# Spreading a relative-position bias over the query rows: four copies out of one SBUF partition, or one round trip through DRAM

## The chip, the cores and the metric

The kernel runs on one core of a Trainium2 chip. The metric is the device time of one execution in microseconds (us), lower is better. Engines are called as the profile calls them: PE is the matrix engine (PEld its weight loads), DVE the vector engine, ACT the scalar engine, POOL the general one, SP the engine that only issues transfers (SPq is its queue). A DMA is a transfer; its landing is the moment at which its completion is signalled.

## The reference

A small model is computed in one launch: two blocks of width 1024 over 256 tokens, about 210 MB of float32 weights. What matters here is the first mixer, a differential attention with 4 heads. Its scores get a bias that depends on the distance of query and key alone:

```python
buckets = t5_bucket(jnp.arange(S, dtype=jnp.int32))
bias_dist = rel_bias.astype(jnp.float32)[buckets].T          # [4 heads, 256 distances]
...
dist = qpos[:, None] - kpos[None, :]
causal = dist >= 0
bias = bias_dist[:, jnp.clip(dist, 0, S - 1)]
s = jnp.einsum('bqhd,bkhd->bhqk', q, k).astype(jnp.float32) * scale + bias
s = jnp.where(causal, s, -jnp.inf)
```

Two such softmaxes (of two halves of each head) are subtracted from each other with a factor lambda, and the result weights the values. Everything after it (cross-attention, MLP, a gated convolution, the second block) is left as it is by the change.

## The kernel before

**Products.** Each activation and each weight is split into two float32r parts, hi and lo, and each product is three matmuls of 128x256: `hi*x_hi`, `hi*x_lo`, `lo*x_hi` (`mm3`, L192; all matmuls stand on L189). A `pair` (L487) is 2 blocks of 128 output features by 8 blocks of depth, so 48 matmuls, from one weight tile of 1 MB.

**The stream of weights.** A list fixed at build time (`plan`) holds all tiles in the order of their use: for the first mixer q, k, q, k (tiles 0 to 3), u, u (tiles 4, 5), v, v (6, 7), then those of the cross-attention's keys. A tile is loaded by SP into one of four staging buffers (`stg`, L297), cast to `hi` by ACT in two halves (L319), and DVE subtracts `lo = stg - hi`, also in halves (L198, in `prep_next`). When DVE has read a staging buffer, SP may load the tile four places later into it. PE and SP run in the order in which the program is written; the order on DVE, ACT and POOL is set by a scheduler at build time.

**SP's queue.** All loads of this kernel but two small ones are issued by SP, one after the other. An issue that has to wait (for a buffer, for data, or for the completion of the eighth DMA before it, whose semaphore it reuses) holds back all that stand behind it.

**The prologue** (`setup`, L342) issues x, tiles 0 to 3, the memory (`memr`, twice 512 KB), the pooling weights (`poolw`) and small constants, and then, in `diff_setup`, the bias. That function takes a one-hot table (`oh`, 33 x 384, loaded in `diff_load`) and multiplies it with `rel_bias` on PE, which gives a row of 384 values for each head: at place j the bias of distance 255 - j, and -1e30 from place 256 on. DVE copies it to SBUF as `be` (L574, 4 partitions, one for each head). Query row p of a head needs 256 values that begin at place 127 - p. So for each head one DMA reads 128 overlapping stretches of 1 KB out of the one partition that holds the head's row, and writes one to each of the 128 partitions of `bias` (L576 to L580):

```python
for h in range(4):
    row = e[h:h + 1, :]
    nc.sync.dma_start(
        out=self.bias[:, h, :],
        in_=bass.AP(row.tensor, row.offset + P - 1, [list(row.ap[0]), [-1, P], [1, T]]))
```

**The use.** `diff_scores` (L598) is called for heads 0 and 1 after the fourth tile's product, for heads 2 and 3 later. For each of two softmaxes and two stretches of keys (256 for the second half of the queries, 128 for the first) one DVE instruction adds the bias to the scores in PSUM and takes the maximum (L613, 16 of them in all, 4 for a head). ACT takes the exponentials, DVE normalises and subtracts (L623 to L630). Then PE turns the weights (`diff_T`, L635 to L637), ACT copies them to SBUF as `pt` (L639), and `diff_out` multiplies them with the values.

**Beside it** POOL forms window sums of `pu`, which DVE writes from the u products (L198 `pu<-g,r`); their temporaries `pwt` share two buffers (tag `sq`) with `pt`, so `pt` of the first head waits until POOL is done with them.

**PE's order** around this place: q, k, q, k, scores of heads 0 and 1 (`a<-dqk`), the two u pairs, a small mean, the first v product, `diff_T` of head 0, the scores of head 2, `diff_out` of head 0, and so on.

Of the kernel before, what the change touches and what calls it, by code (L numbers as in the profile page):

```python
# [10 lines left out]
F32 = mybir.dt.float32  # L11
# [6 lines left out]
P = 128  # L18
# [12 lines left out]
# columns of the table of parameter vectors, 128 values to a column  # L31
# [15 lines left out]
# matrices of weights, cut into tiles of k blocks of 128 rows by n columns  # L47
# [8 lines left out]
def _tiles(a, k, n):  # L56
    """[layers, rows, columns] to [layers, row tile, column tile, partition, k * n]"""
    l, r, c = a.shape
    a = a.reshape(l, r // (k * P), k, P, c // n, n).transpose(0, 1, 4, 3, 2, 5)
    return np.ascontiguousarray(a).reshape(l, r // (k * P), c // n, P, k * n)  # L60


def _layout(inputs):
    """weights by tiles, activations and parameter vectors with features on partitions"""
    out = {}
    for name, (k, n) in TILES.items():
        a = np.asarray(inputs[name])
        if name == "w_in_2":
            gate = a[:, :, 4 * 512:4 * 512 + P]
            out["w_in_2_ff"] = _tiles(gate, k, P)  # L70
            a = np.concatenate([a[:, :, :2048], a[:, :, 2056:]], axis=2)
        out[name] = _tiles(a, k, n)
    # the modulation's weights with output features on partitions
    a = np.asarray(inputs["w_ada_2"])[0].T.reshape(24, 2, P, D)
    out["w_ada_2"] = np.ascontiguousarray(a.transpose(0, 2, 1, 3)).reshape(24, P, 2 * D)
    out.update(_vectors(inputs))
    out["rel_bias"] = np.ascontiguousarray(inputs["rel_bias"])
    out["pool_w"] = np.ascontiguousarray(np.asarray(inputs["pool_w"])[0].transpose(1, 0, 2))
    return out
# [17 lines left out]
def _constants():  # L97
    eye = np.eye(P, dtype=np.float32)
    blk = np.zeros((P, P), np.float32)
    blk[:64, :64] = 1.0 / 64  # L100
    blk[64:, 64:] = 1.0 / 64
    inv = np.zeros((P, 4, 16), np.float32)
    for g, w in enumerate((2, 4, 8, 16)):
        inv[:, g, :] = np.float32(1) / np.minimum(np.arange(16) + 1, w).astype(np.float32)
    small = np.concatenate([eye, blk, inv.reshape(P, 64)], axis=1)

    n = np.arange(T)
    nf = np.maximum(n, 1).astype(np.float32)
    large = 16 + (np.log(nf / np.float32(16)) / np.float32(math.log(8.0))
                  * np.float32(16)).astype(np.int32)  # L110
    bucket = np.where(n < 16, n, np.minimum(large, 31))
    onehot = np.zeros((33, 384), np.float32)
    for j in range(384):
        if j < 256:
            onehot[bucket[255 - j], j] = 1.0
        else:
            onehot[32, j] = NEG

    pos = np.arange(T, dtype=np.float32)
    inv_freq = np.float32(10000.0) ** (-np.arange(0, P, 2, dtype=np.float32) / np.float32(P))  # L120
    ang = (pos[None, :] * inv_freq[:, None]).astype(np.float32)
    cos = np.cos(ang).astype(np.float32)
    sin = np.sin(ang).astype(np.float32)
    rope = np.concatenate([np.concatenate([cos, cos]), np.concatenate([-sin, sin])], axis=1)
    dec = np.zeros((P, 4, T), np.float32)
    for h in range(4):
        lg = math.log(1.0 - 2.0 ** (-5.0 - h))
        d = np.arange(T)[None, :] - np.arange(P)[:, None]
        dec[:, h, :] = np.where(d >= 0, np.exp(np.maximum(d, 0) * lg) * P ** -0.5, 0.0)
    sel = np.zeros((P, 8), np.float32)  # L130
    for h in range(8):
        for part in range(3):
            sel[32 * part + h, h] = 1.0
    mask = np.where(np.arange(P)[:, None] >= np.arange(P)[None, :], 0.0, -(2.0 ** 100))
    late = np.concatenate([rope, dec.reshape(P, 4 * T), sel, mask], axis=1)
    return {"k_small": small.astype(np.float32), "k_onehot": onehot,
            "k_late": late.astype(np.float32)}


class Operand:  # L140
    """an activation, features on partitions, as the sum of two float32r parts"""
# [16 lines left out]
class Kernel:  # L158
# [53 lines left out]
    def w(self, key, name, l, c0, ncol):  # L212
        """256 columns at a time of a matrix of 1024 rows"""
        for c in range(c0 // T, (c0 + ncol) // T):
            self.order.append((key, self.a[name][l, 0, c], 256, 8))
# [33 lines left out]
    def plan_ada(self, start, j, span, n=12):  # L249
        """n loads of the modulation's weights among the items from start"""  # L250
# [34 lines left out]
    def dma_next(self, part=None, parts=4):  # L285
        """the next weights from DRAM, all of them or a part"""
# [131 lines left out]
    def norm_mean(self, acc, parts=False):  # L418
        """mean of squares over D, on every partition: PSUM [P, T]"""
# [11 lines left out]
    def rsqrt(self, out, m, scratch, scale=1.0, gain=1.0, eps=EPS):  # L431
        """out = gain * (scale * m + eps) ** -0.5: a guess by exp and ln, and one Newton step"""
# [31 lines left out]
    def norm_columns(self):  # L464
        """1 / 16 of the norm's scale as columns by token: [P, 2]"""
# [7 lines left out]
    def r_columns(self, r, c=None):  # L473
        """r [P, T], the same on every partition, as columns by token: [P, 2]"""
# [11 lines left out]
    def pair(self, key, x, ko=False, bank=None, start=True, stop=True, k0=0, k1=8, w=None,  # L486
             mid=None):  # L487
        """two blocks of 128 output features: [P, 2, T]"""
# [12 lines left out]
    def halves(self, key, x, k0):  # L501
        """four pairs: the blocks of x from k0 for all of them first, then the others"""
# [10 lines left out]
    def natural(self, key, x, w=None):  # L513
        """[token, 2, 256 output features] with tokens on partitions"""
# [14 lines left out]
    def residual(self, i, v, col, last_norm=None):  # L529
        """h += v for pair i, then the next module's operands"""  # L530
        hp = self.h[:, 2 * i:2 * i + 2, :]
        self.tt(hp, v, hp, ALU.add)
        self.make_x(i, hp, col)
        self.norm_add(i, hp)

# [31 lines left out]
    def diff_setup(self):  # L567
        """the bias by distance, then its band for every query row; lambda"""
# [7 lines left out]
        for h in range(4):  # L576
            row = e[h:h + 1, :]
            nc.sync.dma_start(
                out=self.bias[:, h, :],
                in_=bass.AP(row.tensor, row.offset + P - 1, [list(row.ap[0]), [-1, P], [1, T]]))  # L580
# [17 lines left out]
    def diff_scores(self, h):  # L598
# [11 lines left out]
        spans = ((slice(0, 256), slice(0, 256)), (slice(256, 384), slice(128, 256)))  # L610
        for j in range(2):
            for b, (c, bc) in enumerate(spans):
                nc.vector.tensor_tensor_reduce(out=e[:, j, c], in0=bks[j][:, c],  # L613
                                               in1=self.bias[:, h, bc], op0=ALU.add, op1=ALU.max,
# [64 lines left out]
    def pool_windows(self):  # L679
        """means over windows, less the token itself"""  # L680
# [7 lines left out]
    def pool_step(self, i):  # L688
        """the windows of pair i of the groups"""
# [368 lines left out]
    def ada_row(self):  # L1058
        """silu(c) on every partition"""
# [20 lines left out]
    def shift_cols(self, part):  # L1080
        """the shift as one more column of the operand (and a column of zeros)"""
# [9 lines left out]
    def z_block(self, v, r, dst, bcol):  # L1091
        """dst = v * r, and what the shift adds to it as a column"""
# [30 lines left out]
    def last_of_first(self, i, v):  # L1123
        """the end of the first block: h, and operands for both norms that follow"""
# [6 lines left out]
    def norm_double(self):  # L1131
        """r1 of the final norm, and r12 = r1 * r2, r2 of the norm of what the first gives:
        r2 = (r1 * r1 * m2 + eps) ** -0.5, so r12 = (m2 + eps * (m1 + eps)) ** -0.5"""
# [15 lines left out]
    def two(self, key, x, ko=False, bank=None, mid=None):  # L1149
        """two blocks of output features, each [P, T + 2] in its own bank"""  # L1150
# [11 lines left out]
    def head_rms(self, qk, i, bcol, gain):  # L1162
        """rms over the 64 features of a head, two heads to a block; pair i of qk in place"""
# [16 lines left out]
    def forget(self, v, r):  # L1180
        """cumulative log forget gates, in three bf16 parts whose sum is exact"""
# [9 lines left out]
        # ln(1 + a): a guess, and one Newton step l + (1 + a) * exp(-l) - 1  # L1191
# [15 lines left out]
    def to_natural(self, v2, r, dst, c0):  # L1207
        """two blocks with features on partitions to tokens on partitions: dst [P, 2, c0:c0+2P]"""
# [29 lines left out]
    def gate(self, v2, r, dst, silu):  # L1238
# [6 lines left out]
        # -1 / (1 + exp(-z)): a guess by exp and ln, and one Newton step  # L1245
# [44 lines left out]
    def weighted(self, bk, pt, v, cs, start, stop):  # L1290
        """rows of queries: bk [P, 2, n] from weights pt (keys on partitions) and v"""
# [4 lines left out]
    def fox_out(self, g, pts):  # L1296
        """heads 2g and 2g+1"""
# [13 lines left out]
    def mix_scale(self, o, rr, n):  # L1311
        """o (tokens on partitions, n heads) times rr"""
# [17 lines left out]
    def mix_gate(self, vs, i, part, gname, gates):  # L1330
        """turned heads, times gain and gate: pair i of a part of the operand"""
# [41 lines left out]
    def second_mixer(self):  # L1373
# [84 lines left out]
        # what goes between the two blocks of a pair, and what after it  # L1458
# [92 lines left out]
    def finish(self, i, v):  # L1551
        """the last residual, and out"""
# [75 lines left out]
```

## Time and profile before

| what | value |
|---|---|
| runs of the kernel before | 1122.46, 1122.86, 1123.25 us, median 1122.86 |
| the profiled execution | span 1120.5 us from its first to its last instruction, on core 0 |
| median of the runs less that span | 2.4 us |
| PE busy | 1094.8 us, 98% of the span |
| DVE, ACT, POOL busy | 772.2, 579.5, 122.8 us (69%, 52%, 11%) |
| moved by DMA | 217.75 MB, mean 194 GB/s |

The page gives of the profiled execution its span alone; the runs were timed apart from it, and their median is 2.4 us longer than the span, which is what lies around it. A time taken out of the span or added to it is carried over to the median as it is. PE is busy nearly all the time, but a PE that is busy can still run at either of two clock levels, which the profile gives as the granted clock (1.00 or 0.50).

### The profile page before, as it was taken

What the parts mean: (1) busy time and instruction counts of PE and PEld (TensorE: products, weight loads), DVE (VectorE), ACT (ScalarE), POOL (GpSimd) and SP (SyncE); (2) the same over time, 40 slices, a digit from 0 to 9 for tenths busy, and PEclk for the clock granted to TensorE, in tenths of its full rate; (3) what the DMA queues carried; (4) which work ended last, traced back from release to release, by engine and by line L of the source; (5) the groups of instructions that cost most, each with busy time, mean ns of one, the idle gap of its engine ahead of it and who ended that gap; (6) DMA issues with size and microseconds to landing.
All of it is one profiled execution on the core that took longest, in us unless ns stands there. A gap on an engine that the chain in (4) does not pass through costs nothing.

```text
span 1120.5 us, 21438 instructions
## 1 busy us (share of the span) xinstructions
PE 1094.8 (98%) x9043; PEld 1084.8 (97%) x9043; DVE 772.2 (69%) x1173; ACT 579.5 (52%) x934; POOL 122.8 (11%) x113
## 2 busy tenths in 40 slices
PE   7789999999999999999999999999999999999998
PEld 6689999999999999999999999999999999999998
DVE  6497666886666686674659877656986679555552
ACT  6465554654444464454546544446766657544441
POOL 4130100200000020110001000003222012111110
PEclk9899999999999999999999999999999999999999
DMA  8845454487666555555428877644543335545521
GB/s 254 234 156 186 147 192 145 164 324 256 251 255 256 220 181 188 188 189 188 151 77 334 320 288 275 256 153 171 189 151 114 113 114 197 217 177 183 178 103 39
DMA packets 32747, 217.75 MB, mean 194 GB/s; under 512 B 3683, under 2 KB 4748, under 8 KB 7308
## 3 DMA queue, kind: packets, MB, share of 16 engines
q1 hardware_dynamic: 32560, 216.34, 54.2%
q8 instruction: 71, 1.16, 0.4%
q14 instruction: 24, 0.20, 0.1%
q10 hardware_dynamic: 92, 0.05, 0.0%
HBM read 214.80 MB, written 1.05 MB: 193 GB/s over the span
## 4 chain that ended last, share of the span: by engine, by line
PE 90%; DVE 4%; DMA 3%; ACT 1%; POOL 1%; issue 1%; SPq 0%; DVEq 0%; ACTq 0%; POOLq 0%
PE g L189 59%; PE a L189 30%; DMA stg<-in_ab_w_in_dram 2%; DVE lo L198 2%; DVE xl L201 1%; POOL pwt L198 1%; ACT hi L319 1%; DMA h<-in_xT_dram 0%; POOL acc L198 0%; ACT sq L205 0%; PE a L873 0%; DVE h L201 0%; DVE h L198 0%; PE a L1220 0%; PE a L1326 0%
## 5 line engine op out<-in xcount | busy, mean ns | idle before, releaser
L198 DVE TENSOR_TENSOR lo<-stg,hi 128x1024 fp32r<-128x1024 f32 (+1 forms) x356 | 437.9, 1246 | 182.3 <-ACT hi L319 179.3
L319 ACT CAST hi<-stg 128x1024 fp32r<-128x1024 f32 (+1 forms) x356 | 361.8, 1039 | 387.4 <-PE g L189 212.8
L189 PE MATMUL g<-xh,hi 128*128 128x256 f32 (+1 forms) x1408 | 402.6, 286 | 7.9 <-ACT hi L319 7.6
L189 PE MATMUL g<-xh,lo 128*128 128x256 f32 (+1 forms) x1408 | 399.3, 284 | 1.5 <-DVE lo L198 1.5
L189 PE MATMUL g<-xl,hi 128*128 128x256 f32 (+1 forms) x1408 | 398.1, 283 | 0.8 <-DVE xl L201 0.8
L189 PEld LDWEIGHTS g<-xh,hi 128*128 128x128 f32 x1408 | 267.3, 190 | 10.9 <-ACT hi L319 9.3
L189 PEld LDWEIGHTS g<-xl,hi 128*128 128x128 f32 x1408 | 268.1, 190 | 2.2 <-DVE xl L201 1.0
L189 PEld LDWEIGHTS g<-xh,lo 128*128 128x128 f32 x1408 | 267.5, 190 | 2.6 <-DVE lo L198 2.6
L189 PE MATMUL a<-uh,lo 128*128 128x256 f32 x800 | 226.4, 283 | 0.0
L189 PE MATMUL a<-uh,hi 128*128 128x256 f32 x800 | 226.3, 283 | 0.0
L189 PE MATMUL a<-ul,hi 128*128 128x256 f32 x800 | 226.3, 283 | 0.0
L189 PEld LDWEIGHTS a<-uh,lo 128*128 128x128 f32 x800 | 152.7, 191 | 0.0
L189 PEld LDWEIGHTS a<-ul,hi 128*128 128x128 f32 x800 | 152.6, 191 | 0.0
L189 PEld LDWEIGHTS a<-uh,hi 128*128 128x128 f32 x800 | 152.6, 191 | 0.0
L189 PE MATMUL g<-uh,hi 128*128 128x256 f32 x288 | 81.7, 284 | 0.0
L189 PE MATMUL g<-ul,hi 128*128 128x256 f32 x288 | 81.5, 283 | 0.0
L189 PE MATMUL g<-uh,lo 128*128 128x256 f32 x288 | 81.5, 283 | 0.0
L198 POOL TENSOR_TENSOR acc<-sq 128x256 f32<-128x256 f32 x10 | 7.9, 791 | 545.0 <-ACT sq L205 369.0
L1066 DVE CUSTOM_DVE_ANT_0 stg<-stg,crow 128x1024 f32<-128x1024 f32 x48 | 57.5, 1220 | 5.6 <-DMA stg<-in_w_ada_dram 5.4
L189 PEld LDWEIGHTS g<-uh,lo 128*128 128x128 f32 x288 | 55.2, 192 | 0.0
L189 PEld LDWEIGHTS g<-ul,hi 128*128 128x128 f32 x288 | 55.2, 192 | 0.0
L189 PEld LDWEIGHTS g<-uh,hi 128*128 128x128 f32 x288 | 55.2, 192 | 0.0
(300 smaller groups left out, 1369.7 us busy)
## 6 DMA issues: line engine op xcount, KB each, us to landing
stg<-in_mlp_w_dram SPq DMA_DIRECT2D x64, 1024.0 KB, 5.0
stg<-in_w_ada_dram SPq DMA_DIRECT2D x24, 1024.0 KB, 5.2
stg<-in_xattn_wkv_dram SPq DMA_DIRECT2D x16, 1024.0 KB, 4.8
stg<-in_w_in_dram SPq DMA_DIRECT2D x16, 1024.0 KB, 4.8
stg<-in_w_mlp_in_dram SPq DMA_DIRECT2D x16, 1024.0 KB, 4.8
stg<-in_w_mlp_out_dram SPq DMA_DIRECT2D x16, 1024.0 KB, 4.8
stg<-in_conv_w_in_dram SPq DMA_DIRECT2D x12, 1024.0 KB, 4.9
stg<-in_xattn_wq_dram SPq DMA_DIRECT2D x8, 1024.0 KB, 4.9
```

The costliest lines, as they stand in the source:

```text
L189: self.nc.tensor.matmul(out, lhsT, rhs, start=start, stop=stop, skip_group_check=True)
L198: (eng or self.nc.vector).tensor_tensor(out=out, in0=a, in1=b, op=op)
L201: (eng or self.nc.vector).scalar_tensor_tensor(out=out, in0=a, scalar=s, in1=b, op0=op0, op1=op1)
L319: self.nc.scalar.copy(hi[:, s], t[:, s])
L1066: self.nc.vector.tensor_tensor_reduce(out=t[:, b, :], in0=t[:, b, :], in1=self.c_row, op0=ALU.mult, op1=ALU.add, scale=1.0, scalar=0.0, ac ...
```

## The change

The row of 384 values is now stored the other way round: the one-hot table is turned, so that place i holds the bias of distance i - 127 (and -1e30 where that is negative). `be` is written to a small DRAM tile (4 rows of 384 values, 6 KB, one DMA), and one DMA reads from there the stretches of all 128 query rows and 4 heads, 512 of 1 KB each, and writes them to `bias` (512 KB). Query row p's stretch begins at place p. Since the keys now stand backwards in `bias`, the DVE instruction that adds it reads it with a step of -1, and the stretch of the first 128 queries is the first half of it, not the second. The words between lines of code (comments, docstrings) are gone too, so that lines behind L580 stand 5 further on.

```diff
@@ _constants
         if j < 256:
-            onehot[bucket[255 - j], j] = 1.0
+            onehot[bucket[255 - j], 382 - j] = 1.0
         else:
-            onehot[32, j] = NEG
+            onehot[32, (382 - j) % 384] = NEG
@@ diff_setup
         self.bias = self.act.tile([P, 4, T], F32, tag="ul", name="bias", bufs=2)
-        for h in range(4):
-            row = e[h:h + 1, :]
-            nc.sync.dma_start(
-                out=self.bias[:, h, :],
-                in_=bass.AP(row.tensor, row.offset + P - 1, [list(row.ap[0]), [-1, P], [1, T]]))
+        ed = self.dram.tile([4, 384], F32, name="e_dram")
+        nc.sync.dma_start(out=ed, in_=e)
+        nc.sync.dma_start(out=self.bias, in_=bass.AP(ed.tensor, ed.offset,
+                                                     [[1, P], [384, 4], [1, T]]))
+
+    @staticmethod
+    def backwards(a):
+        n = a.shape[1]
+        return bass.AP(a.tensor, a.offset + n - 1, [list(a.ap[0]), [-1, n]])
@@ diff_scores
-        spans = ((slice(0, 256), slice(0, 256)), (slice(256, 384), slice(128, 256)))
+        spans = ((slice(0, 256), slice(0, 256)), (slice(256, 384), slice(0, 128)))
...
-                                               in1=self.bias[:, h, bc], op0=ALU.add, op1=ALU.max,
+                                               in1=self.backwards(self.bias[:, h, bc]), op0=ALU.add, op1=ALU.max,
```

**How it moves instructions.** PE and POOL keep their order. On SP the place is the end of the prologue. Before, the four copies of the bias stand between the last constant (`small`) and the load of tile 4 (`stg_162`):

```order
L366 DMA poolw<-in_pool_w_dram 128x512
L368 DMA small<-in_k_small_dram 128x320
L578 DMA bias<-be 128x1x256 x4
L297 DMA stg_162<-in_ab_w_in_dram 128x2048
L297 DMA stg_235<-in_ab_w_in_dram 128x2048
```

After the change:

```order
L366 DMA poolw<-in_pool_w_dram 128x512
L368 DMA small<-in_k_small_dram 128x320
L578 DMA e_dram<-be 4x384
L579 DMA bias<-e_dram 128x4x256
L297 DMA stg_161<-in_ab_w_in_dram 128x2048
L297 DMA stg_234<-in_ab_w_in_dram 128x2048
```

Four issues have become two, of which the second waits for the landing of the first; tile 4 (now `stg_161`) and all later loads stand behind that wait.

On DVE the scheduler has changed its order from the fourth product (`dqk`, the second k) to some 100 rows on. The place is where the scores of heads 0 and 1 begin; `lo_328` and `lo_327` are the lo parts of tile 4. Before:

```order
L201 SCALAR_TENSOR_TENSOR dqk<-g_335,r_280 128x512
L198 TENSOR_TENSOR lo_328<-stg_162,hi_327 128x1024 x2
L198 TENSOR_TENSOR dqk<-g_393,r_280 128x512
L613 ISA de_467,dmx_468<-a_470,bias 128x256
L613 ISA dmx_468 128x1
```

After the change:

```order
L201 SCALAR_TENSOR_TENSOR dqk<-g_334,r_279 128x512
L198 TENSOR_TENSOR dqk<-g_392,r_279 128x512
L198 TENSOR_TENSOR lo_327<-stg_161,hi_326 128x1024 x2
L618 ISA de_466,dmx_467<-a_469,bias 128x256
L618 ISA dmx_467 128x1
```

The second k's `dqk`, which waits for PE's fourth product, now stands ahead of tile 4's two lo parts, not behind them.

The third place is some 35 rows further on DVE, at the second `pu`, from which POOL's window sums start (`lo_585` and `lo_584` are the lo parts of tile 7, the second v). Before:

```order
L479 COPY rc_582<-s_579 128x2
L198 TENSOR_TENSOR lo_585<-stg_251,hi_584 128x1024 x2
L198 TENSOR_TENSOR pu<-g_592,r_280 128x2x256
L198 TENSOR_TENSOR lo_688<-stg_333,hi_687 128x1024 x2
```

After the change:

```order
L479 COPY rc_581<-s_578 128x2
L198 TENSOR_TENSOR lo_584<-stg_250,hi_583 128x1024
L198 TENSOR_TENSOR pu<-g_591,r_279 128x2x256
L198 TENSOR_TENSOR lo_584<-stg_250,hi_583 128x1024
L198 TENSOR_TENSOR lo_687<-stg_332,hi_686 128x1024 x2
```

One of the two lo parts of tile 7 has gone behind `pu`.

## Rows read from the trace of the kernel before

**Rows 1.** The page: busy time, share of the span and instructions of each engine.

```profile
PE 1094.8 (98%) x9043; PEld 1084.8 (97%) x9043; DVE 772.2 (69%) x1173; ACT 579.5 (52%) x934; POOL 122.8 (11%) x113
```

**Rows 2.** PE's waits in the whole span: us in total, times, longest.

```profile
PE g L189 <- ACT hi L319: 7.6, 2, 7.3
...
PE a L189 <- ACT pt L639: 4.1, 1, 4.1
PE a L189 <- DVE xl L201: 1.7, 2, 0.9
```

**Rows 3.** The chain that ended last, 25 to 75 us: start, us, what.

```profile
25.77 17.17 DMA stg<-in_ab_w_in_dram
43.02 1.05 ACT hi L319
...
60.77 0.61 DVE pu L198
...
61.45 1.56 POOL pwt L198
...
69.47 0.49 ACT pt L639
```

**Rows 4.** Timeline of SP's queue, 14 to 26 us: start, us of the issue, what.

```profile
14.53 11.14 SPq L578 DMA_DIRECT2D bias<-be  x4
25.77 7.95 SPq L297 DMA_DIRECT2D stg<-in_ab_w_in_dram  x1
```

**Rows 5.** By stretches: length, busy PE, PEld, DVE, ACT, POOL; granted clock, DMA share, GB/s.

```profile
20.00:21.00 1.00, 1.00 (x9) 0.94 (x8) 0.54 (x1) 0.25 (x1) 0.00 (x0) 1.00 1.00 394
...
24.00:25.00 1.00, 1.00 (x11) 1.00 (x10) 1.00 (x2) 1.00 (x2) 0.00 (x0) 1.00 0.77 24
...
41.00:42.00 1.00, 0.00 (x0) 0.00 (x0) 0.00 (x0) 0.00 (x0) 0.00 (x0) 0.50 0.99 410
```

**Rows 6.** DMA issues: KB each, us to landing (x1: the first bias copy, at 14.53).

```profile
bias<-be SPq DMA_DIRECT2D x4, 128.0 KB, 17.5
bias<-be SPq DMA_DIRECT2D x1, 128.0 KB, 12.7
out_dram<-h SPq DMA_DIRECT2D x3, 256.0 KB, 2.4
stg<-in_w_out_dram SPq DMA_DIRECT2D x4, 1024.0 KB, 4.9
crow<-c_dram SPq DMA_DIRECT2D x2, 512.0 KB, 5.8
```

**Rows 7.** A stretch while `crow` is read (columns as in rows 5).

```profile
216.00:217.00 1.00, 1.00 (x11) 1.00 (x10) 1.00 (x2) 0.94 (x3) 0.03 (x1) 1.00 1.01 361
```

**Rows 8.** Timeline of DVE: start, us, instruction, idle time before it and its releaser.

```profile
44.10 2.36 DVE L198 TENSOR_TENSOR lo<-stg,hi 128x1024 fp32r<-128x1024 f32 x2 [13.89 <-ACT hi L319]
46.38 0.68 DVE L198 TENSOR_TENSOR dqk<-g,r 128x512 f32<-128x512 f32 x1
46.98 0.41 DVE L613 CUSTOM_DVE_ANT_0 de<-a,bias 128x256 f32<-128x256 f32 x1
60.70 0.68 DVE L198 TENSOR_TENSOR pu<-g,r 128x512 f32<-128x512 f32 x1
```

**Rows 9.** Timeline of PE, 35 to 70 us (columns as in rows 8).

```profile
35.11 1.68 PE L189 MATMUL a<-dqk 64*128 64x256 f32 x16
44.12 0.58 PE L189 MATMUL g<-xh,hi 128*128 128x256 f32 x1 [7.33 <-ACT hi L319]
52.68 0.36 PE L189 MATMUL g<-xh,hi 128*128 128x256 f32 x1
58.46 0.59 PE L189 MATMUL a<-acc,mean 128*128 128x256 f32 x2
65.00 0.93 PE L189 MATMUL a<-dqk 64*128 64x256 f32 x8
70.00 1.65 PE L189 MATMUL a<-dvu,pt 128*128 128x128 f32 x6 [4.07 <-ACT pt L639]
```

## The prediction

> **What bounds the kernel now.** I read the busy shares first: PE is busy 98% of the span [rows 1], so time can only be won where PE stands still or runs slow. PE's waits in the whole span come next: one of 7.3 us for ACT's `hi`, one of 4.1 us for `pt`, and, past the start of the program, little else of one piece [rows 2]. Both lie between 35 and 70 us. Then I followed the chain that ended last through that stretch. It runs from one load of a weight tile, which takes 17.17 us from its issue at 25.77, over ACT's cast to DVE, on DVE to the second `pu` at 60.7, over POOL's window sums to `pt` at 69.5, and from there to PE [rows 3]. From 70 us on PE hardly waits: what is left in its list after the two is 1.7 us and less [rows 2]. So a shift of the start of `diff_out` at 70.00 [rows 9] reaches the end of the kernel unshortened.
>
> Why does that load take 17 us, when one of the same size takes 4.9 with the queue free [rows 6]? SP's queue shows the four bias copies issued from 14.53 on, over 11.14 us, and right behind them tile 4, whose issue alone lasts 7.95 us [rows 4]. The stretches show what the transfer engines did meanwhile: 394 GB/s until about 21 us, while the prologue's loads flow; then 24 GB/s at a busy share of 0.77; and 410 GB/s again once the bias is through [rows 5]. The copies out of one partition keep the engines occupied at a sixteenth of the rate, and tile 4 stands behind them. DVE is idle for 13.89 us for want of tile 4's `hi` [rows 8] and PE for 7.33 us [rows 9].
>
> **The change, part by part.**
>
> *The four copies go.* They land 17.5 us after issue (the median [rows 6]). What they leave is a free queue from about 22 us on.
>
> *The write of `be` to DRAM* (4 rows, 6 KB) takes the first copy's place in the queue at 14.53. No row shows it. From below, the output stores at the quiet end land 2.4 us after issue [rows 6], which gives 16.9. From above, the first bias copy, which stood at the same place with more to move, landed 12.7 us after issue [rows 6], which gives 27.2. The loads ahead of it are through when the rate falls, between 20 and 24 us [rows 5]. I take 22 + 2.4 = 24.4.
>
> *The load of the bias from DRAM* waits for that landing, and so do tile 4 and all loads behind it on SP. The nearest row is `crow`, which spreads 4 KB of DRAM over 128 partitions, 512 KB in all, and lands in 5.8 us [rows 6] at 361 GB/s [rows 7]. It differs in its pieces, 4 KB there and 1 KB here. From below, 512 KB at 410 GB/s is 1.3 us; from above, at the 24 GB/s of the old copies it is 21.8 us. I take `crow`: issue 24.5, landing 30.3.
>
> [...]
>
> *Tile 4* is issued about 1 us behind the bias load, so at 25.5, no earlier than before. It lands 4.9 us after issue with a free queue, plus 1.4 us for the 512 KB ahead of it: 31.8. With the upper end for the write it is 34.6. PE wants it at 35.11 + 1.68 = 36.8 [rows 9], less ACT's cast of 1.05 [rows 3], so at 35.7. At both ends the tile is off the path.
>
> *DVE's path.* The second k's `dqk` now stands first. PE's fourth product ends as the scores begin, at 35.1 [rows 9], so `dqk` runs from 35.2 and takes 0.60 (46.38 to 46.98). The two lo parts of tile 4 take 2.28 (44.10 to 46.38, 1.14 each), and the scores begin at 38.1, not at 46.98. From there to the second `pu` DVE took 13.72 us (46.98 to 60.70) [rows 8]. One lo part of 1.14 is now behind `pu`, so 12.58: `pu` at 50.7, not 60.7. From `pu` to `diff_out` the chain takes 9.30 us [rows 3, 9], over POOL. I leave it as it is, since DVE is as dense beside it: `diff_out` at 60.0, not 70.0.
>
> *PE's path* must be no later. It begins the u products at 36.8 and waits 0.2 for the first lo part. A u product takes 5.78 (52.68 to 58.46), the first with a small transpose 5.9; mean, v and `diff_T` take 6.54 (58.46 to 65.00), the next scores 0.93 [rows 9]. That is 36.8 + 0.2 + 5.9 + 5.8 + 6.5 + 0.9 = 56.1. So PE stands 3.9 us before 60.0 as it stood 4.07 before 70.00, and the wait for `pt` stays. The first u product ran 8.56 us with the clock at its lower level (0.50 in the wait before it [rows 5]), and that loss vanishes too, but inside this second wait: it pays nothing.
>
> *The backward reading* on DVE: 16 instructions. No row reads with a negative step. From below it costs nothing (a gain has no reason: the same elements are read). From above it doubles them: the 8 of heads 0 and 1, of at most 0.41 each [rows 8], cost 3.3 us on the path. I take nothing, since the nearest rows are these instructions themselves.
>
> *No cost:* the turned one-hot table (same size), two issues fewer on SP.
>
> **Sum.** 70.0 - 60.0 = 10.0 us off the span of 1120.5. The median of the runs is 2.4 us above that span, and the difference carries over: 1122.9 - 10.0 = 1112.9.
>
> **The rivals.**
>
> *A: a smaller gain.* The backward reading costs (up to 3.3), or tile 4 comes a little after 34.7, when DVE wants it cast. For: neither is shown by a row. Against: the reserve of 2.9 us on tile 4. It gives 1114.5 to 1117.5.
>
> *B: a larger gain.* POOL's sums run quicker, or their wait is short enough for PE's clock to stay up. POOL's first `pwt` takes 1.56 us in this chain [rows 3]; without any wait PE would go on at 56.1, which is 13.9 us and the lowest end: 1109.0. Against: DVE runs the same work beside POOL.
>
> *C: no change.* Tile 4 lands as late as before, at 42.9, because the write of `be` or the wait on it lasts to about 35, or the new load doesn't spread as its 128 rows say. [...] Against: the first bias copy's 12.7 us bounds a far larger transfer at that place. 1122.9.
>
> *D: slower.* All 512 pieces come out of the same 6 KB of DRAM, so one place of the memory may serve them one after another. At the old rate of 24 GB/s the load takes 21.8 us, from 24.5 to 46.3, tile 4 behind it another 2.6 (1 MB at 410 GB/s) to 48.9, where it landed at 42.9 before: 6 us slower, 1128.9. It decides from 15.8 us for the bias load on (24.5 + 15.8 + 2.6 = 42.9), or 33 GB/s. Against it stands `crow`, a still smaller source, at 361 GB/s [rows 7]. [...]
>
> **How the numbers follow.** The forecast (1111 to 1114.5) gets 0.70, A 0.14, B 0.06, C 0.04, D 0.06. From 1109.0, the end of B, to 1117.5, the end of A with its unknown costs, 0.90 is held; I keep that, since the walk along DVE's order was done by hand over 25 us, and an unseen wait there would fall anywhere in it. About 0.2%, 2.2 us, is what a measurement of this kernel can tell from no change. Forecast, A and B are faster: 0.90. C is the same, 0.04; D slower, 0.06.
>
> **What would show it.** In the new profile the load of tile 4 should still be issued at 24 to 26 us and land at 31 to 35; the rate should fall to near nothing for about 2 us before 25 (the landing of 6 KB) and then be over 300 GB/s. PE's wait for `hi` near 37 should be gone, its wait for `pt` of about 4 us should stand at 56 to 60, and `diff_out` begin near 60. DVE's instructions with the bias (256 wide) should take 0.41 us as before; if they take twice that, A is right. The forecast is wrong if the bias load lasts over 8 us (then tile 4 comes late), or if a wait of PE turns up behind 60 us that wasn't there.

## The result, and the profile after

| kernel | runs | median of runs (lowest to highest) | ratio to the kernel before, 95% interval |
|---|---|---|---|
| before | 4 groups of runs, one beside each set below | 1122.71, 1123.08, 1123.31, 1122.85 us | |
| changed | 4 | 1114.18 us (1113.66 to 1115.74) | 0.9925 [0.9911, 0.9939] |
| changed, on another occasion | 4 | 1114.22 us (1113.65 to 1114.71) | 0.9923 [0.9908, 0.9938] |

The change makes the kernel 8.5 us faster. 10.0 us were forecast, 1112.9 us. In the profiled execution the span went from 1120.5 to 1112.2 us, 8.3 us. (The execution profiled here took 1114.0 us, 1.8 more than its span. So not all of the 2.4 us named ahead of the prediction lies around the span; about 0.6 of it comes from a profiled execution quicker than the median. The differences don't depend on it.) I read the views of the changed kernel in the order in which those of before stand above.

The page, busy time of each engine (answers to [rows 1]):

```profile
PE 1093.1 (98%) x9043; PEld 1083.5 (97%) x9043; DVE 770.3 (69%) x1173; ACT 578.7 (52%) x934; POOL 125.0 (11%) x113
```

The work is the same; 8 us of standing still are gone, and they don't show in a share of 98%. PE's waits from 26 to 110 us (answers to [rows 2]):

```profile
PE a L189 <- ACT pt L644: 5.5, 1, 5.5
```

The 7.3 us for `hi` have left the list, as forecast. The wait for `pt` has not stayed at 4.1 but grown to 5.5. SP's queue, 12 to 45 us (answers to [rows 4]), and from the DMA view the time of the bias load from issue to landing:

```profile
14.28 0.33 SPq L578 DMA_DIRECT2D e_dram<-be  x1
23.45 0.39 SPq L579 DMA_DIRECT2D bias<-e_dram  x1
23.94 3.14 SPq L297 DMA_DIRECT2D stg<-in_ab_w_in_dram  x4
```

```profile
bias<-e_dram SPq DMA_DIRECT2D x1, 512.0 KB, 4.2
```

SP stands 9 us until the 6 KB are in DRAM; then the bias load, tile 4 and three more tiles go out within 4 us. By stretches (columns as in rows 5):

```profile
21.00:22.00 1.00, 1.00 (x11) 1.00 (x10) 0.39 (x1) 0.97 (x3) 0.00 (x0) 1.00 0.87 322
...
23.00:24.00 1.00, 1.00 (x10) 1.00 (x11) 0.97 (x3) 1.00 (x3) 0.00 (x0) 1.00 0.03 12
24.00:25.00 1.00, 1.00 (x11) 1.00 (x10) 1.00 (x4) 1.00 (x3) 0.10 (x1) 1.00 0.08 30
25.00:26.00 1.00, 1.00 (x11) 1.00 (x10) 1.00 (x2) 0.67 (x2) 0.92 (x2) 1.00 0.89 303
...
27.00:28.00 1.00, 1.00 (x10) 1.00 (x10) 1.00 (x3) 0.00 (x0) 0.92 (x2) 1.00 1.03 409
```

Before, the transfer engines were 77% busy at 24 GB/s [rows 5]. Now they are nearly empty (0.03) while the row lands, and then the bias flows at 303 GB/s with tile 4 right behind it at 409. Timelines of ACT and DVE, 28 to 56 us (start, us, instruction, idle time before it and its releaser; answers to [rows 8]):

```profile
30.19 2.00 ACT L319 CAST hi<-stg 128x1024 fp32r<-128x1024 f32 x2 [1.39 <-DMA stg<-in_ab_w_in_dram]
```

```profile
34.63 0.69 DVE L198 TENSOR_TENSOR dqk<-g,r 128x512 f32<-128x512 f32 x1 [5.01 <-PE g L189]
35.24 2.35 DVE L198 TENSOR_TENSOR lo<-stg,hi 128x1024 fp32r<-128x1024 f32 x2
37.51 0.42 DVE L618 CUSTOM_DVE_ANT_0 de<-a,bias 128x256 f32<-128x256 f32 x1
...
50.22 0.68 DVE L198 TENSOR_TENSOR pu<-g,r 128x512 f32<-128x512 f32 x1
50.83 3.48 DVE L198 TENSOR_TENSOR lo<-stg,hi 128x1024 fp32r<-128x1024 f32 x3
54.23 0.41 DVE L201 SCALAR_TENSOR_TENSOR rsq<-a,rsq 128x256 f32<-128x256 f32 x1
```

Tile 4 has landed at 30.2, not at 42.9. DVE follows the forecast closely: scores at 37.5 (38.1 forecast), the second `pu` at 50.2 (50.7). The instruction that reads the bias backwards takes 0.42 us, where forwards it took 0.41 [rows 8]. From here on things differ. POOL of the changed kernel, and below it POOL and DVE of the kernel before at the same place:

```profile
50.98 3.82 POOL L198 TENSOR_TENSOR pwt<-pu 128x271 f32<-128x271 f32 x1 [3.76 <-DVE pu L198]
54.88 1.50 POOL L198 TENSOR_TENSOR pwt<-pwt 128x269 f32<-128x269 f32 x1
```

```profile
61.45 1.55 POOL L198 TENSOR_TENSOR pwt<-pu 128x271 f32<-128x271 f32 x1 [4.30 <-DVE pu L198]
63.08 1.50 POOL L198 TENSOR_TENSOR pwt<-pwt 128x269 f32<-128x269 f32 x1
```

```profile
61.30 4.37 DVE L198 TENSOR_TENSOR lo<-stg,hi 128x1024 fp32r<-128x1024 f32 x3
```

The same POOL instruction takes 3.82 us instead of 1.55, and the three `lo`s that DVE runs beside it take 3.48 instead of 4.37. I read that as POOL coming in between them before, so that DVE paid; now DVE runs through, and POOL waits until DVE turns to `rsq` at 54.23 and ends at 54.80. So this step costs 2.27 us more. From `pu` to `diff_out` the loss is 1.45 only, since POOL's later steps were quicker, above all the fourth, here in the kernel before and in the changed one:

```profile
66.10 1.61 POOL L198 TENSOR_TENSOR pwt<-pu 128x271 f32<-128x271 f32 x1
```

```profile
58.09 0.81 POOL L198 TENSOR_TENSOR pwt<-pu 128x271 f32<-128x271 f32 x1
```

PE, 34 to 70 us (answers to [rows 9]):

```profile
34.52 1.68 PE L189 MATMUL a<-dqk 64*128 64x256 f32 x16
...
36.13 0.38 PE L189 MATMUL g<-xh,hi 128*128 128x256 f32 x1
...
54.53 0.93 PE L189 MATMUL a<-dqk 64*128 64x256 f32 x8
...
60.97 1.65 PE L189 MATMUL a<-dvu,pt 128*128 128x128 f32 x6 [5.51 <-ACT pt L644]
...
69.82 0.83 PE L189 MATMUL a<-dvu,pt 128*128 128x128 f32 x6
```

`diff_out` begins at 60.97 instead of 70.00, 9.03 earlier. The second `diff_out`, at 69.82, stood before at

```profile
78.11 0.83 PE L189 MATMUL a<-dvu,pt 128*128 128x128 f32 x6
```

which is 8.29 earlier: 0.74 was lost between the two. The granted clock shows where. Stretches of the changed kernel, then of the kernel before:

```profile
58.00:60.00 2.00, 0.00 (x0) 0.00 (x0) 2.00 (x11) 0.00 (x0) 1.84 (x4) 0.68 0.95 291
60.00:62.00 2.00, 1.03 (x5) 1.04 (x6) 0.81 (x2) 1.42 (x2) 1.32 (x2) 0.50 0.90 377
62.00:64.00 2.00, 2.00 (x11) 2.00 (x11) 0.69 (x2) 1.35 (x8) 0.00 (x0) 0.50 0.01 4
64.00:66.00 2.00, 2.00 (x13) 2.00 (x13) 2.00 (x8) 2.00 (x9) 0.00 (x0) 0.62 0.00 0
```

```profile
70.00:72.00 2.00, 2.00 (x10) 2.00 (x10) 2.00 (x10) 1.20 (x3) 0.39 (x1) 0.50 0.74 311
72.00:74.00 2.00, 2.00 (x16) 2.00 (x15) 2.00 (x7) 1.77 (x9) 0.00 (x0) 0.77 0.00 0
```

In the kernel before PE works at the lower level from 70.00 to about 72.9 (0.77 of 72 to 74 is 0.92 us at 0.50); now, behind a wait of 5.51 and not 4.07 us, from 60.97 to about 65.5. That is 4.5 us against 2.9. At that level the changed kernel's matmuls of 128x256 begin 0.21 us apart (63.3 to 65.2 us), at the upper one 0.12 (66 to 68), so 0.7 us more is lost. The account closes: `pu` 10.48 earlier (60.70 to 50.22), less 1.45 on POOL's way, is 9.03; less 0.74 at the lower clock, 8.29; the span says 8.3.

### The profile page after: what moved, and what is told of

Read it like the earlier page. It is cut to its first block, busy times and chain, and to the rows that moved or that the text cites. A ratio compares the mean times of both kernels' runs of the same rounds, so it can differ in the third digit from the quotient of the medians.

```text
span 1112.2 us, 21431 instructions
## 1 busy us (share of the span) xinstructions
PE 1093.1 (98%) x9043; PEld 1083.5 (97%) x9043; DVE 770.3 (69%) x1173; ACT 578.7 (52%) x934; POOL 125.0 (11%) x113
## 4 chain that ended last, share of the span: by engine, by line
PE 92%; DVE 4%; POOL 1%; ACT 1%; issue 1%; DMA 0%; SPq 0%; DVEq 0%; POOLq 0%; ACTq 0%
PE g L189 61%; PE a L189 30%; DVE lo L198 2%; DVE xl L201 1%; POOL pwt L198 1%; POOL acc L198 1%; ACT hi L319 1%; DMA stg<-in_ab_w_in_dram 0%; ACT sq L205 0%; PE a L878 0%; DVE h L201 0%; DVE h L198 0%; ACT xh L205 0%; DVE de L632 0%; PE a L1331 0%
```

## The experiments

### What the removed copies cost

**e2_partition_backward** undoes the source alone; the bias is still read backwards:

```diff
-        ed = self.dram.tile([4, 384], F32, name="e_dram")
-        nc.sync.dma_start(out=ed, in_=e)
-        nc.sync.dma_start(out=self.bias, in_=bass.AP(ed.tensor, ed.offset,
-                                                     [[1, P], [384, 4], [1, T]]))
+        for h in range(4):
+            row = e[h:h + 1, :]
+            nc.sync.dma_start(out=self.bias[:, h, :],
+                in_=bass.AP(row.tensor, row.offset, [list(row.ap[0]), [1, P], [1, T]]))
```

> The changed kernel with its turned table and backward reading, but the bias again by four copies out of one SBUF partition each. Theory (the source of the copies is what counts): tile 4 lands near 43 us as in the kernel before, PE waits about 7.3 us for it, and the time is that of before, 1121.5 to 1124. Rival (the turned order of the keys, or DVE's backward reading, has a part in the gain or costs something): it lands between, 1115 to 1120, or above 1125 with DVE's instructions of the bias longer than 0.42 us.

1122.96 us, ratio 0.9999 [0.999, 1.0008]. A stretch of it:

```profile
24.00:25.00 1.00, 1.00 (x11) 1.00 (x10) 1.00 (x3) 1.00 (x3) 0.05 (x1) 1.00 0.75 25
```

It is the kernel before again: 25 GB/s, a wait of 8.2 us for `hi`. So the turned table, the copies' direction and DVE's step of -1 are worth nothing that these runs could tell (within 1.1 us either way), and the gain comes from the way in which the row reaches `bias`. One thing more went back in this run: the scheduler gave DVE the order of the kernel before, with tile 4's `lo`s ahead of the last `dqk` and both of tile 7's ahead of the second `pu`. The next run shows that the new order isn't needed for the gain.

**e7_sbuf_wide** keeps four copies from SBUF to SBUF of the same sizes, out of 128 partitions instead of one; what they copy is a piece of the activation `h`, so the position bias and the causal mask are left out:

```diff
-            row = e[h:h + 1, :]
-            nc.sync.dma_start(out=self.bias[:, h, :],
-                in_=bass.AP(row.tensor, row.offset + P - 1, [list(row.ap[0]), [-1, P], [1, T]]))
+            nc.sync.dma_start(out=self.bias[:, h, :], in_=self.h[:, h, :])
```

> The kernel before, in which the four copies into the bias have the same size and the same 128 pieces of 1 KB, and SBUF as their source, but read x, piece p from partition p; the position bias and the causal mask are thereby left out of the computation. Theory (one partition as the source is slow, not SBUF and not 1 KB pieces): the copies run at over 250 GB/s, tile 4 is issued before 24 us and lands before 30, PE's wait of 7.3 us is gone, 1112 to 1115. Rival (small pieces, or SBUF to SBUF, are slow as such): tile 4 lands near 43 and the time stays at 1121 to 1124.

1111.31 us, ratio 0.9897 [0.988, 0.9913], a little below what was expected. Its stretches:

```profile
22.00:23.00 1.00, 1.00 (x10) 1.00 (x10) 0.85 (x1) 0.97 (x4) 0.00 (x0) 1.00 0.97 303
23.00:24.00 1.00, 1.00 (x11) 1.00 (x10) 0.97 (x4) 1.00 (x3) 0.00 (x0) 1.00 0.83 254
```

In these stretches other loads flow beside the copies (tile 4 is issued at 22.01), so the rate isn't theirs alone. What it costs the engines can be told all the same: 254 GB/s at a share of 0.83 of the 16 engines is 0.054 us of an engine for each KB, the other loads' among them, and 24 at 0.77 [rows 5] is 0.53. By this estimate the same 512 pieces, SBUF on both sides, are about ten times as quick when the source lies on 128 partitions. (In the packets of the traces a piece of 1 KB takes 0.50 us in the kernel before and 0.046 in the changed kernel, both medians.) So neither "SBUF to SBUF" nor the size of the pieces was the matter, but a source of one partition for each copy. What this run doesn't separate: its pieces also lie apart, while those of the row overlap and begin every 4 bytes. Pieces that overlap so are quick out of DRAM (303 GB/s); out of SBUF they were tried from one partition alone. What in a source of one partition sets the 24 and 25 GB/s, no run here tells.

This run is also faster than the changed kernel by 2.9 us (2.4 in the profiled executions). Tile 4 is cast from 29.25 instead of 30.19, but that isn't what it gains by: its second `pu` comes only 0.5 us earlier. DVE has the order of the kernel before, and POOL's step is the short one:

```profile
50.50 1.55 POOL L198 TENSOR_TENSOR pwt<-pu 128x271 f32<-128x271 f32 x1 [4.30 <-DVE pu L198]
```

and from its second `pu` (49.74) to `diff_out` (59.04) it takes 9.30 us, what the forecast had assumed.

**e5_load_twice** and **e5_load_four_times** leave the change in place and delay tile 4 by something else: the bias load is issued two or four times in a row.

```diff
-        nc.sync.dma_start(out=self.bias, in_=bass.AP(ed.tensor, ed.offset, ...
+        for _ in range(4):
+            nc.sync.dma_start(out=self.bias, in_=bass.AP(ed.tensor, ed.offset, ...
```

> Edit: the changed kernel with the load of `bias` issued twice in a row on SP, the second waiting for the first (same places, same bytes). Tile 4 is so issued about 4.2 us later, and lands at 34 to 35 instead of 30.1. The planned order of DVE puts all the scores of the first two heads ahead of tile 4's `lo`. Theory (what counts is only when tile 4 comes, and it had a reserve of some 4 us ahead of DVE's last `dqk`): landing itself costs nothing, the order of DVE costs what the scores hold up `lo`: the product u starts at 39 to 40 instead of 36.1, and the time is 1115 to 1118.5. Rival (no reserve: each us of the load counts): 1118 to 1119.5. Rival (the load does not count at all): 1113.5 to 1115.

> Edit: the load of `bias` issued four times in a row, each waiting for the one before. Tile 4 is issued about 12.6 us later, near 36.5, and lands near 43, where the kernel before had it landed by way of the one-partition copies. Theory (the lateness of tile 4 alone is what the copies cost, whatever brings it about): PE waits for `hi` of tile 4 for 6.5 to 8.5 us and the time is that of the kernel before within 2.5 us, 1120.5 to 1125.5. Rival (the copies cost something else too, their reads of SBUF beside the engines for one): clearly below, 1117 to 1120.

1115.91 us (0.9934 [0.9919, 0.9949]) and 1120.63 us (0.9978 [0.9969, 0.9987]). PE at the first u product, twice and four times:

```profile
39.37 0.39 PE L189 MATMUL g<-xh,hi 128*128 128x256 f32 x1 [2.52 <-ACT hi L319]
```

```profile
42.84 0.58 PE L189 MATMUL g<-xh,hi 128*128 128x256 f32 x1 [6.15 <-ACT hi L319]
```

With the start of the first u product at 36.1 (the changed kernel), 39.4, 42.8 and 44.1 us [rows 9] the times are 1114.2, 1115.9, 1120.6 and 1122.9 (the starts can shift by about 1 us with the prologue of the profiled execution). Both runs fall into what the theory gave, the second by 0.1 us, but they delay more than the tile: DVE and ACT now have all the scores and the first exponentials of heads 0 and 1 ahead of tile 4. With two loads the tile has landed at 35.5 (issued at 29.09, 6.4 us to landing), and ACT casts it only at 38.28, so most of the 2.5 us that PE waits for it are the order's and not the load's. The time rises by 1.7 us only; the wait for `pt` is 2.6 us in this run, not 5.5. The run with four is the better test of a late tile: it lands at 41.0 (34.60 and 6.4 us) and ACT casts it from 41.8, not from 43.0 [rows 3], since the loads took 3.7 us each, not 4.2. It lies 2.7 us below the kernel before beside it (1123.31), so about 6 of the 8.5 us are gone again without any copy out of one partition.

### Why 1.3 us of the forecast are missing

**e12_pu_one_lo_later** and **e14_other_ops_behind_pu** change what DVE runs behind the second `pu`. The first moves `pu` behind one more `lo`:

```diff
+            with self.tc.high_priority(-80 * i):
-            self.tt(self.pu[:, 2 * i:2 * i + 2, 16:], v, self.bc2(r), ALU.mult)
+                self.tt(self.pu[:, 2 * i:2 * i + 2, 16:], v, self.bc2(r), ALU.mult)
```

The second puts tile 8's `lo`s off:

```diff
-            parts, later = (2, PREP_LATER) if i else (4, 0)
+            parts, later = (2, 250 if i in (8,) else PREP_LATER) if i else (4, 0)
```

> Edit: the changed kernel with the second `pu` given a later place on DVE, behind one more `lo` (128x1024, 1.14 us); everything else on DVE stands in the same order, so two `lo`s and not three follow `pu` before `rsq`, an operation of another form. Theory A (POOL's first step is held for as long as DVE goes from one `lo` to the next, and gets in when DVE turns to `rsq`): `pu` ends 1.1 us later, POOL's first step takes about 2.7 us instead of 3.82 and ends at the same time, diff_out starts at 61.0 as in the changed kernel, 1113.5 to 1115 us. Theory B (POOL gets in after the first of the `lo`s when that is the first half of a tile, as it did in the kernel before): 1.5 to 1.8 us for POOL's first step, diff_out near 59.9, 1112 to 1113.5 us. Theory C (POOL's 3.82 us has nothing to do with these `lo`s): POOL's step stays near 3.8 us, diff_out 62, 1114.5 to 1116 us.

> Edit: the changed kernel with tile 8's `lo`s given a later place, so that on DVE one `lo` follows the second `pu`, then four short operations on pair 0 of the pooling (`dvu`, two of 128x240 and two of 128x32), and then the next `lo`. Theory (POOL's first step behind `pu` is held while DVE runs `lo`s back to back): it ends when the one `lo` does, at 1.7 to 2.0 us, and the chain of POOL behind it has its 9.0 to 9.5 us from `pu` to diff_out (59.3 to 59.8); later `lo`s cost PE up to 1 us elsewhere: 1111.5 to 1113.5 us. Rival (the hold comes from POOL's own side, or from the transfers): 3.8 us again and 1114 to 1115.5 us. Rival (the `lo`s put off are late for PE): diff_out earlier, but 1114 us or more.

> The changed kernel itself beside the two others, on the same chip. All theories: 1114.2 us within 1, POOL's first step behind the second `pu` at 3.8 us again. If it is at 1.5 to 2 us here, the hold is a matter of chance from run to run and no step of the account may rest on it.

1114.41 us (0.9922 [0.9906, 0.9939]), 1115.89 us (0.9937 [0.9922, 0.9952]) and, for the changed kernel again, 1114.22 us. POOL's first step behind `pu` in e12, e14 and e15:

```profile
53.12 2.69 POOL L198 TENSOR_TENSOR pwt<-pu 128x271 f32<-128x271 f32 x1 [4.89 <-DVE pu L198]
```

```profile
50.50 1.91 POOL L198 TENSOR_TENSOR pwt<-pu 128x271 f32<-128x271 f32 x1 [3.75 <-DVE pu L198]
```

```profile
50.99 3.82 POOL L198 TENSOR_TENSOR pwt<-pu 128x271 f32<-128x271 f32 x1 [3.76 <-DVE pu L198]
```

Three `lo`s in a row hold it for 3.82 us, two for 2.69, less by 1.13, the time of a `lo`; with one, and other operations behind it, it is 1.91. What theory A of e12 said of this kernel holds, and the 3.82 is no matter of chance from run to run, since e15 repeats it. (In e12's profile `diff_out` begins at 62.0, not 61.0: DVE's last `dqk` begins 1.0 us later too, at 35.63.) Theory B falls: in e12 the first `lo` behind `pu` is the first half of a tile, and POOL does not get in. In e14 the time from `pu` (49.75) to `diff_out` (59.65) is 9.90 instead of 10.75, less won than the 1.9 us at the first step, since its later steps ran longer (the last two `pwt` 2.46 us, where they took 1.42 in the changed kernel). Its time, 1111.5 to 1113.5 expected, was missed: the last rival's price came, a wait of PE for a `lo`:

```profile
PE g L189 <- DVE lo L198: 2.1, 1, 2.1
```

So this order is no improvement, and shows how little slack the `lo`s have.

**e10_load_act_queue** issues the bias load on ACT's queue, so that tile 4 need not wait for the row:

```diff
-        nc.sync.dma_start(out=self.bias, in_=bass.AP(ed.tensor, ed.offset,
+        nc.scalar.dma_start(out=self.bias, in_=bass.AP(ed.tensor, ed.offset,
```

> Edit: the changed kernel with the load of `bias` from `e_dram` issued on ACT's queue instead of SP's, so that it is ACT and not SP that stands until `e` has landed; tile 4's load stands on SP right behind the write of `e`. The planned order of DVE changes with it: `lo` of tile 4 and one half of tile 5's stand ahead of the scores (tile 4's ahead of the last `dqk`), and all of tile 6's ahead of the second `pu`. Theory (what the changed kernel lost against the forecast is three `lo`s run back to back right behind the second `pu`, beside which POOL's first step took 3.82 us instead of 1.55): tile 4 lands by 29, `bias` by 31, the idle time ahead of the last `dqk` holds tile 4's `lo`; POOL's first step behind `pu` takes under 2 us, `pu` to diff_out is 9.0 to 9.6 us again, and the time is that of the run with the wide SBUF source, 1110 to 1112.5 us. Rival (POOL's 3.82 us has nothing to do with what DVE runs beside it, or DVE is as late with another order): no more than 1 us below the changed kernel, 1113 to 1115. Second rival: ACT, standing at the load until `e` has landed, is late with its casts and tile 4 gains nothing: 1114 to 1117.

1110.63 us, ratio 0.9884 [0.987, 0.9899], so better than the changed kernel by 3.6 us. DVE, POOL and PE:

```profile
29.69 2.91 DVE L198 TENSOR_TENSOR lo<-stg,hi 128x1024 fp32r<-128x1024 f32 x2 [0.16 <-ACT hi L319]
34.54 0.69 DVE L198 TENSOR_TENSOR dqk<-g,r 128x512 f32<-128x512 f32 x1 [1.94 <-PE g L189]
```

```profile
50.63 1.55 POOL L198 TENSOR_TENSOR pwt<-pu 128x271 f32<-128x271 f32 x1 [4.30 <-DVE pu L198]
```

```profile
58.04 1.65 PE L189 MATMUL a<-dvu,pt 128*128 128x128 f32 x6 [2.82 <-ACT pt L644]
```

Tile 4's `lo`s fill DVE's idle time ahead of the last `dqk`, POOL's step is the short one, and from `pu` (49.87) to `diff_out` it takes 8.17 us, even less than the 9.0 to 9.6 expected. ACT's casts were not held up: it issued the load at 28.09, behind a square that had waited for POOL, and cast tile 4 from 28.62. The bias landed 6.2 us after issue, at 34.3 and not by 31, which was still ahead of the first scores (36.28). But here two `lo`s follow `pu`, as in e12, and POOL came in after the first of them. So theory A doesn't carry over to this kernel, and what decides whether POOL comes in between two `lo`s is not settled:

| kernel | `lo`s in a row behind `pu` | POOL's first step, us | `pu` to `diff_out`, us |
|---|---|---|---|
| before | 3 | 1.55 | 9.30 |
| e7_sbuf_wide | 3 | 1.55 | 9.30 |
| changed, e15 | 3 | 3.82 | 10.75 |
| e12_pu_one_lo_later | 2 | 2.69 | 9.6 |
| e10_load_act_queue | 2 | 1.55 | 8.17 |
| e14_other_ops_behind_pu | 1 | 1.91 | 9.90 |

The other kept traces fit no simple rule either: POOL's first step took 1.55 in e2 and in both e5 runs, 1.49 in the two runs below that are called e4 and e11, and 3.75 in e3. What the five runs in which it was held longer (the changed kernel, e15, e3, e12, e14) share is the changed kernel's order on DVE up to the place of the second `pu`; that this is the reason was not tested.

### What the wait for `pt` is worth, and a faster kernel

**e3_after_own_buffers** and **e4_before_own_buffers** give POOL's temporaries two buffers of their own, so that `pt` need not wait for them, in the changed kernel and in the kernel before.

```diff
-                    dst = self.sm.tile([P, n], F32, tag="sq", name=self.nm("pwt"))
+                    dst = self.sm.tile([P, n], F32, tag="acc", name=self.nm("pwt"), bufs=2)
```

> The changed kernel; POOL's window temporaries take the two buffers of the norm accumulators and no longer those of pt. Theory (after the change PE's wait for pt, 5.5 us, and the low clock behind it, some 4.5 us long at half speed, are what the chain over POOL costs): the wait is gone, diff_out begins near 55.5 to 56.5 us, and the time is 1106 to 1109. Rival (the wait is handed on: DVE's work for the heads or the pooled values come late elsewhere): 1111 to 1114.

> The kernel before with the same change of POOL's buffers alone. Theory: its wait for pt (4.1 us) and a low clock of 2.9 us at half speed behind it are gone, 1116 to 1119, and the distance to the changed kernel with these buffers is 10 to 11 us, more than the 8.5 us between the kernels as they were, since the difference was lost in POOL's chain and in the clock. Rival (the missing 1.5 us of the forecast were lost elsewhere): the distance stays at 8.5 us or less.

1109.75 us, ratio 0.9884 [0.9869, 0.9898], and 1123.56 us, ratio 1.0005 [0.9996, 1.0015]. Both missed, the first by little. The distance between the two is 13.8 us, which neither the theory (10 to 11) nor the rival (8.5 or less) had. PE in the changed kernel with own buffers:

```profile
56.81 0.94 PE L189 MATMUL a<-dvu,pt 128*128 128x128 f32 x6 [0.94 <-ACT pt L644]
63.57 0.83 PE L189 MATMUL a<-dvu,pt 128*128 128x128 f32 x6
69.75 0.39 PE L189 MATMUL g<-meml,hi 128*128 128x256 f32 x1 [1.44 <-DVE meml L198]
```

The second `diff_out` comes 6.25 us earlier than in the changed kernel (69.82), but the time falls by 4.4 only: behind it PE waits for DVE, 1.44 us in the last line. In the kernel before the same edit brings nothing:

```profile
67.23 0.94 PE L189 MATMUL a<-dvu,pt 128*128 128x128 f32 x6 [0.94 <-ACT pt L639]
71.47 0.47 PE L635 MATMUL a<-small,de 128*128 128x128 f32 x1 [3.30 <-DVE dmx L613]
79.96 0.83 PE L189 MATMUL a<-dvu,pt 128*128 128x128 f32 x6
```

Here DVE, 10 us late since tile 4, takes the scores of head 2 at 70.8 only, and the 3.1 us won at `pt` come back as 3.3 us of waiting for it. The two changes don't add: own buffers are worth 4.4 us behind the change and nothing ahead of it.

**e11_act_queue_own_buffers** puts e10 and e3 together.

> Edit: as e10_load_act_queue, and POOL's partial sums have two buffers of their own as in e3_after_own_buffers. Theory: the gains are of two kinds and only partly add, since the second half of e3's gain was handed on to DVE: pt is waited for under 1.5 us, the wait of diff_T for DVE's scores is smaller than in e3, time 1106 to 1109 us, below each alone. Rival (both take away the same wait, so that nothing adds): the time of e3 within 1 us, 1109 to 1110.5. Rival that the next limit is another (the `mem` operand on DVE, the norm): not below e3, 1110 to 1112.

1108.78 us, ratio 0.9881 [0.9863, 0.9899], single runs from 1108.35 to 1112.5. PE:

```profile
56.16 0.94 PE L189 MATMUL a<-dvu,pt 128*128 128x128 f32 x6 [0.94 <-ACT pt L644]
63.93 0.94 PE L189 MATMUL a<-dvu,pt 128*128 128x128 f32 x6 [0.81 <-ACT pt L644]
```

It lies in the theory's range, but its interval covers those of e3 and e10, so these runs don't show that it is better than either. All three are faster than both the kernel before and the changed one.

## Why the prediction was right, and where it was off

**What bounds the kernel: right.** The path over tile 4, DVE, `pu`, POOL and `pt` set the time, and e5 with four loads shows it by delaying the tile (the bias itself is late too, and DVE waits 2.9 us for it).

**The copies go: right.** e2 (1122.96 us with sources of one partition) and e7 (1111.31 with 128) show that the source of one partition was their price, with the reservation made at e7.

**The write of `be`: right.** Landed by 23.45, 24.4 forecast. SP's wait behind it was the forecast's main unknown, and it landed after the prologue's loads were through, between 21 and 23 us.

**The bias load: right, a little quicker.** 4.2 us instead of the 5.8 of `crow`. Pieces of 1 KB, read out of 6 KB of DRAM, ran at 303 GB/s. Rival D, one place of the memory serving all 512 pieces at 24 GB/s, is out: it needed 15.8 us.

**Tile 4: right, a little early.** Issued at 23.94 and landed at 30.2, just ahead of the 24 to 26 and the 31 to 35 that were to show it (31.8 forecast); the reserve ahead of DVE was 4 us.

**DVE to `pu`: right.** 10.48 us earlier against 10.0, by the order of its instructions and durations from the rows of before.

**The backward reading: right.** 0.42 us for 256 keys in the changed kernel and in e2, 0.41 before. The upper bound of 3.3 us and with it one half of rival A is out.

**From `pu` to `diff_out`: the step that failed.** The prediction said "I leave it as it is, since DVE is as dense beside it" and took 9.30. It measured 10.75. DVE was just as dense, but that did not fix the price: the durations add up as if only one of POOL's step and DVE's `lo`s ran at a time, and which of them waited had turned. In the kernel before the `lo`s took 4.37 and POOL's step 1.55; now 3.48 and 3.82. POOL's later steps gave back 0.8 of the 2.27 us that its first one lost. Why it turned stays open. That one waited for the other is my reading of these durations. What the traces show is that POOL's step lasted past two `lo`s in e12 and three here, and ended 0.58 and 0.57 us after DVE had turned to `rsq` (55.81 against 55.23, and 54.80 against 54.23), where the quickest such step took 0.63 as a whole.

**"Reaches the end of the kernel unshortened": off by 0.74.** The shift was carried on whole but for the clock: PE did 4.5 us of work at the lower level and not 2.9. That the longer wait is the reason is not shown: waits of 2.8, 3.2 and 4.1 us (e10, e7, the kernel before) were followed by 3.0, 3.4 and 2.9 us of work at that level.

Together 1.45 + 0.74 against 0.48 that DVE gave more than forecast make 8.29 out of 10.0, and the median agrees with 8.5. That the time still fell within the range is in part luck. The median lies 0.3 us below its upper end (1114.5), one of the four runs (1115.74) above it, and the losses of 1.45 and 0.74 had no term in the sum; the 1.6 us of room above the forecast was not worked out for them. Of the rivals A's time came nearest (1114.5 to 1117.5, where its own 3.3 us would end at 1116.2), though not by its mechanism; B's thought that POOL's sums could run at another pace was right, with the other sign.

## What to carry to other kernels

Where a small table is spread over all partitions, look at the partitions of the source, not at "SBUF or DRAM": here the copies out of one partition held up everything queued behind them (tile 4 landed at 42.9 us, without them at 30.2), and their price could be read from the GB/s of the stretch beside a high busy share (24 at 0.77). When a path is moved whole to another place in time, the steps beside which another engine works can't safely be carried over with their old durations, even if that engine does the same work (POOL's step went from 1.55 to 3.82 us); put both orders of who waits into the range. Before buffers are spent on a wait, ask what stands behind it: the same two buffers were worth 4.4 us in one kernel and nothing in the other.

## What the runs showed of the hardware

- A source of one SBUF partition gave 24 and 25 GB/s for pieces of 1 KB, and kept the transfer engines 77 and 75% busy with it, 0.50 us for a piece (the median, in the kernel before); out of 6 KB of DRAM that 512 overlapping pieces read, a piece took 0.046 us (the median), and the load ran at 303 GB/s; with copies out of 128 partitions, other loads beside them, the rate was 254 and 303 GB/s.
- The custom DVE instruction of the scores, with two f32 inputs, takes the same time within 0.01 us when one is read with a step of -1 (0.42 and 0.28 us for 256 and 128 columns).
- A POOL addition of 128x271 took 0.63 us at its quickest, and 1.55, 1.91, 2.69 or 3.82 beside one to three DVE subtractions of 128x1024. Whether it gets in between two of them came out the same in both profiles of the changed kernel (3.82; the other kernels have one profile each), but what decides it was not found.
